# A decoder trunk layer: both feed-forwards by seven products, with the first one's side work cut into steps and its state-space matrices built on GpSimd

## The chip, the cores and the metric

The kernel runs on one core of one Trainium2 chip. The metric is the device time of one execution, in microseconds (us). Engines are called as the profile calls them: PE is TensorE (PEld its weight load), DVE VectorE, ACT ScalarE, POOL GpSimd, SP SyncE, which issues most of the DMAs.

## The reference

One layer with D = 1024, a prompt of 1024 tokens and eight samples of 8 tokens. A feed-forward stands ahead of the token mixer and another behind it:

```python
def swiglu(u, w_in, w_out):
    g, up = jnp.split(u @ w_in, 2, axis=-1)
    return (jax.nn.silu(g) * up) @ w_out
...
    mod = jax.nn.silu(c) @ lp['ada_w'] + lp['ada_b']
    sh1, sc1, g1, sh2, sc2, g2, sh3, sc3, g3 = jnp.split(mod, ADA_CHUNKS, axis=-1)
    h = x + 0.5 * g1[:, None, :] * swiglu(rms_modulate(x, lp['norm_ffn1'], sh1, sc1),
                                          lp['ffn1_w_in'], lp['ffn1_w_out'])
    mix, k, v, sr, si = token_mixer(rms_modulate(h, lp['norm_mix'], sh2, sc2), lp, attend, s0_re, s0_im)
    h = h + g2[:, None, :] * mix
    h = h + 0.5 * g3[:, None, :] * swiglu(rms_modulate(h, lp['norm_ffn2'], sh3, sc3),
                                          lp['ffn2_w_in'], lp['ffn2_w_out'])
```

The mixer has stick-breaking attention and a diagonal complex state-space model (SSM) of 32 groups, 16 channels and 64 states each. The powers and products of the SSM's parameters don't depend on x, so that the kernel can build them at any time before the mixer.

## The kernel before, in words

**Layout.** Activations lie transposed: 1024 features are 8 k-tiles of 128 partitions, and T = 1092 columns hold the prompt, the samples and 4 columns of padding, worked as three chunks of 364 or two halves of 546. Each fp32 product is three f16 passes (high by high, high by low, low by high). A weight block is 1 MB. Class `Weights` fetches it on SP's queue into one of two `wf` buffers, measures it (`absmax`, L89, on DVE, then `partition_all_reduce`, L82, on POOL, then a power of two, L74 to L76), and splits it: the high half on ACT (L101), the low half on DVE (L102). `one_ahead` splits the weights of the next block and loads those of the one after.

**A feed-forward** has 22 inner tiles of 128, in three parts: 0 to 9, 10 to 17, 18 to 21. An *up block* makes one inner tile h (gate and up product, SiLU, product of both). After the up block 10, `down(0)` multiplies the tiles 0 to 9 by their rows of `w_out` and adds to x; then come the up blocks 11 to 21, `down(1)`, and `last_part`.

**The first feed-forward** (`ffn`) uses plain up blocks: `unit` (L216), 144 matmuls of 364 columns. Tiles 0 and 1 are made by chunks beside the modulation of x (`up_two`). x stays in SBUF, and `down` adds to it. Its `fill` puts work of others between the blocks: `ada_part` for the parts 2 to 8 of the modulation, one in each of the blocks 0 to 6 (eight 512 KB weight tiles, issued on POOL's queue at L285, then 32 narrow matmuls at L289); `reload`, which fetches x again; `prep0`, the SSM's parameters, at block 8; and `ssm_prep(bt)` for the four quarters of the SSM's matrices at the blocks 13, 15, 17 and 19, with its elementwise work on DVE (`cmul`, L766 to L775, and L937). Its tiles share one pool `hp` of 15 slots with h.

**The second feed-forward** (`ffn_seven`) makes only the tiles 0 to 3 by plain blocks (`halves_unit`, L242). For the other 18, it cuts weights (256 inner columns) and u into 2x2 quarters and takes seven products of quarters, in place of eight, with sums formed before and after (`seven_products`, L455: 168 matmuls of 272 or 274 columns). The sums of the weights are made on DVE (`seven`, L162 to L165), those of u once, by `Factors.sums` (L430, L431), from the fp32 values kept in x's space. x itself goes to DRAM (`xd`); `down(0)` fetches it row by row and writes it back, and after the last up block it is loaded whole into u's space.

**Order.** The framework plans the program when it is built: each engine's instructions stand then in one fixed order. A tile whose pool is full waits for the release of a slot.

Of the kernel before, what the change touches and what calls it, by code (L numbers as in the profile page):

```python
# [20 lines left out]
P = 128  # L21
# [10 lines left out]
CH = 364  # L32
# [60 lines left out]
def abs_bound(k, src, out):  # L93

    junk = k.tmp().rearrange("p a n -> p (a n)").bitcast(BF16)[:, :src.shape[1]]
    k.nc.scalar.activation(junk, src, AF.Abs, accum_out=out)
# [9 lines left out]
class Weights:  # L106
# [48 lines left out]
    def seven(self, f, s):  # L155
# [4 lines left out]
        t, t4 = (k.tmp().rearrange("p a n -> p (a n)") for _ in range(2))  # L160
        s3, s2, s4 = t[:, :512], t[:, 512:1024], t4[:, :512]
# [115 lines left out]
def ada_part(k, dr, part, queue=None, then=None):  # L277

    nc = k.nc
    ps = k.pss.tile([P, 256], F32, tag="s")  # L280
    for kk in range(2):
        ws = []
        for i in range(4):
            wt = k.hp.tile([P, 4, 256], F32, tag="h", name="aw")
            (queue or nc.gpsimd).dma_start(wt, dr["ada_w"][part, kk, i])  # L285
            ws.append(wt)
        for j in range(4):
            for i in range(4):
                nc.tensor.matmul(ps[32 * i:32 * i + 32, :], k.cs[:, 4 * kk + j, :], ws[i][:, j, :],  # L289
                                 start=kk + j == 0, stop=kk == 1 and j == 3)  # L290
        if kk == 0 and then:
# [8 lines left out]
    nc.vector.tensor_tensor(view(k.mods[:, sl, :]), pt[:, :, :, :NSQ],  # L300
                            view(k.ada_b[:, sl].unsqueeze(2).to_broadcast([P, 8, NSQ])), op=ALU.add)

# [108 lines left out]
class Factors:  # L411

    def __init__(self, k, u):
        self.u, self.t = u, []

    def sums(self, k, x, g):
# [15 lines left out]
    def get(self, n):
        if n[0] == "b":
            k0, c0 = 4 * int(n[1] == "2"), HT * int(n[2] == "2")
            return lambda kt, part: self.u[:, k0 + kt, part, c0:c0 + HT]
        i, j = {"t1": (0, 0), "t3": (0, 1), "t2": (1, 0), "t4": (1, 1)}[n]
        return lambda kt, part: self.t[2 * kt + i][:, j, part]


def seven_products(k, w, fac, iv, h, meanwhile):
# [17 lines left out]
    u2 = k.u2.tile([P, HT], F32, tag="u2", bufs=2)  # L460
# [61 lines left out]
def ffn_order(wi, wo, seven=False):  # L522
    o = [(wi[i], KD, 256, *(("seven",) if seven and i >= PLAIN else ())) for i in range(NFF)]
# [6 lines left out]


def ffn(k, x, u, ivu, gate, fill, after_chunk, between=None):

    nc = k.nc
    hs, hm = {}, {}
    act = lambda kt, part: u[:, kt, part, :]

    def up(i):
        w = k.w.next()
        iv = mul_small(k, w[1], ivu)  # L540
        pg = unit(k, w, slice(0, P), act, KD)
        sil = k.tp.tile([P, T], F32, tag="sil", bufs=2)
        nc.scalar.activation(c3(sil), pg, AF.Silu, scale=iv)
        pu = unit(k, w, slice(P, 2 * P), act, KD)
        h = k.hp.tile([P, T], F32, tag="h")
        nc.vector.scalar_tensor_tensor(c3(h), pu, iv, c3(sil), op0=ALU.mult, op1=ALU.mult)  # L546
        p = [a <= i < b for a, b in PARTS].index(True)
        if p not in hm:
            hm[p] = k.small.tile([P, 12], F32, tag="hm", bufs=3)
        j = i - PARTS[p][0]  # L550
        absmax(k, h, hm[p][:, j:j + 1])
        hs[i] = h
        for f in fill.get(i, ()):
            f()

    def up_two():

        ws = [k.w.ready.pop(0) if between else k.w.next() for _ in range(2)]
        ivs = [mul_small(k, w[1], ivu) for w in ws]
        sil = [k.tp.tile([P, T], F32, tag="sil", bufs=2) for _ in range(2)]  # L560
        hm[0] = k.small.tile([P, 12], F32, tag="hm", bufs=3)
        behind = None
        for i in range(2):
            hs[i] = k.hp.tile([P, T], F32, tag="h")
        for c in range(3):
            for i in range(2):
                ps = k.psu.tile([P, 3, 512], F32, tag="u", bufs=k.nunits)
                for q in range(2):
                    product(k, ps[:, q, :CH], ws[i], slice(q * P, q * P + P), act, KD, c)
                a, b = c3(sil[i])[:, c], c3(hs[i])[:, c]  # L570
                with k.tc.issue_after(behind) if behind else nullcontext():
                    g = nc.scalar.activation(a, ps[:, 0, :CH], AF.Silu, scale=ivs[i])
                b = nc.vector.scalar_tensor_tensor(b, ps[:, 1, :CH], ivs[i], a, op0=ALU.mult, op1=ALU.mult)
                behind = between(c, i, g.ins, b.ins) if between else None
        for i in range(2):
            absmax(k, hs[i], hm[0][:, i:i + 1])
            for f in fill.get(i, ()):
                f()

    def halves(p):  # L580
        a, b = PARTS[p]
        s, inv = pow2_scale(k, allmax(k, absmax(k, hm[p][:, :b - a])), tag="sh", bufs=3)
        parts = []
        for i in range(a, b):
            h2 = k.hp.tile([P, 2, T], F16, tag="h")
            ins = split(k, h2[:, 0, :], h2[:, 1, :], hs[i], s)
            if i - a < 6:
                behind = ins
            parts.append(h2)
        return lambda kt, part: parts[kt][:, part, :], inv, behind  # L590

    def down(p, hact, inv, behind):
        nk = PARTS[p][1] - PARTS[p][0]
        per = 1 + p
        for m in range(KD):
            if m % per == 0:
                if m == 0:
                    with k.tc.issue_after(behind):
                        w = k.w.next()
                else:  # L600
                    w = k.w.next()
                iv = mul_small(k, w[1], inv)
            ps = unit(k, w, slice(m % per * P, m % per * P + P), hact, nk)
            add_gated(k, x[:, m, :], ps, scaled_gate(k, gate[:, m, :], iv))

    up_two()
# [1214 lines left out]
```

## Time and profile before

| what | value |
|---|---|
| time, median of 3 runs | 2479.41 us (2475.33 to 2481.81) |
| profiled execution | 2487.87 us, of which the span of the trace is 2485.9 us |
| mean granted TensorE clock | 0.983 of full speed |
| busy share of the span | PE 96%, DVE 63%, PEld 62%, ACT 35%, POOL 7% |

All times of single instructions come from the profiled execution. Stretches are given in microseconds from the span's start. "x" is a count, and what stands in square brackets behind a row of a timeline is the engine's idle time before the instruction and what ended it.

### The profile page before, as it was taken

To read this page: it belongs to the slowest core of one execution; us is meant where nothing else is said; L and a number is where in the kernel's file an instruction comes from. 1 tells how busy PE (TensorE), PEld (TensorE's weight loads), DVE (VectorE), ACT (ScalarE), POOL (GpSimd) and SP (SyncE) were. 2 spreads that over 40 slices of the span, in tenths; PEclk is the share of its full clock that TensorE was granted. 3 is DMA by queue.
4 is the path that set the end of the run, shared out by engine and by line. 5 is a ranking of instruction groups with operands and counts; after the bars stand their busy time and mean duration, and the time that the engine had idled before them with its cause. 6 is when DMAs were issued, how large, how long until landed. Compare 5 with 4: busy or idle time off the path is not lost.

```text
span 2485.9 us, 40892 instructions
## 1 busy us (share of the span) xinstructions
PE 2389.5 (96%) x17575; PEld 1550.6 (62%) x17575; DVE 1558.6 (63%) x2895; ACT 866.8 (35%) x1049; POOL 171.1 (7%) x249
## 2 busy tenths in 40 slices
PE   6999999999999999999999999999999999999997
PEld 2555566666656566685444444556678878888784
DVE  4522373458675753747889787597477645777735
ACT  3311130111122332236677677332433321333303
POOL 0111000000000000001133300000000000000000
PEclk8999999999999999899999999999999999999999
DMA  9654111212121225445233312622111133111302
GB/s 352 216 193 170 33 50 51 68 55 80 70 71 52 100 88 150 119 132 195 70 109 104 97 42 102 219 73 105 42 39 65 33 133 107 61 54 66 124 18 73
DMA packets 88533, 247.45 MB, mean 100 GB/s; under 512 B 12112, under 2 KB 49360, under 8 KB 78112
## 3 DMA queue, kind: packets, MB, share of 16 engines
q1 hardware_dynamic: 74528, 197.85, 23.6%
q0 software_dynamic: 13376, 46.70, 5.4%
q8 instruction: 137, 2.24, 0.4%
q14 instruction: 44, 0.36, 0.0%
q10 hardware_dynamic: 448, 0.29, 0.0%
HBM read 199.62 MB, written 45.19 MB: 98 GB/s over the span
## 4 chain that ended last, share of the span: by engine, by line
PE 39%; DVE 8%; ACT 4%; DMA 2%; issue 2%; another core or an unknown queue 1%; POOL 0%; DVEq 0%; POOLq 0%; ACTq 0%
PE u L455 13%; PE u L242 9%; PE u L226 8%; PE u L216 3%; PE z L1123 2%; PE o L1141 1%; PE P L1060 1%; DVE wl L102 1%; DVE mx L89 1%; PE P L1136 1%; DMA wf<-in_ffn_w_in 1%; DVE h L102 1%; DMA wf<-in_w_in 1%; DMA wf<-in_w_out_b 0%
## 5 line engine op out<-in xcount | busy, mean ns | idle before, releaser
L216 PEld LDWEIGHTS <-wh 128*128 128x128 f16 x3360 | 320.9, 97 | 225.4 <-issue 38.0
L226 PE MATMUL u<-u,wh 128*128 128x364 f16 (+1 forms) x1632 | 392.7, 318 | 11.1 <-ACT u L389 6.3
L216 PE MATMUL u<-u,wh 128*128 128x364 f16 (+1 forms) x2112 | 392.6, 317 | 0.0
L101 ACT ACTIVATE wh<-wf,sc 128x2048 f16<-128x2048 f32 (+2 forms) x110 | 177.3, 1613 | 540.6 <-PE u L216 308.1
L89 DVE TENSOR_REDUCE mx<-wf 128x1 f32<-128x2048 f32 (+2 forms) x116 | 209.9, 1823 | 201.0 <-DMA wf<-in_ffn_w_in 112.6
L226 PE MATMUL u<-u,wl 128*128 128x364 f16 (+1 forms) x816 | 259.7, 318 | 1.1 <-DVE wl L102 1.1
L226 PEld LDWEIGHTS <-wh 128*128 128x128 f16 x1824 | 175.9, 98 | 123.9 <-issue 26.6
L102 DVE SCALAR_TENSOR_TENSOR wl<-wf,sc,wh 128x2048 f16<-128x2048 f32 (+2 forms) x110 | 204.7, 1861 | 50.7 <-ACT wh L101 48.4
L216 PEld LDWEIGHTS <-wl 128*128 128x128 f16 x1680 | 163.3, 98 | 96.8 <-issue 2.8
L216 PE MATMUL u<-u,wl 128*128 128x364 f16 (+1 forms) x1056 | 220.7, 315 | 0.0
L242 PE MATMUL u<-h,wh 128*128 128x274 f16 (+1 forms) x1152 | 184.4, 281 | 8.5 <-ACT h L101 7.8
L82 POOL PARTITION_ALL_REDUCE am<-mx x106 | 52.3, 499 | 1930.4 <-DVE mx L89 1869.2
L216 PE MATMUL u<-h,wh 128*128 128x364 f16 (+1 forms) x864 | 157.3, 317 | 5.2 <-DVE h L102 3.5
L242 PEld LDWEIGHTS <-wh 128*128 128x128 f16 x1408 | 137.5, 98 | 38.4 <-issue 9.5
L226 PEld LDWEIGHTS <-wl 128*128 128x128 f16 x912 | 89.0, 98 | 69.0 <-issue 18.0
L455 PEld LDWEIGHTS <-wh 128*128 128x128 f16 x1152 | 112.9, 98 | 24.4 <-issue 1.1
L546 DVE SCALAR_TENSOR_TENSOR h<-u,iv,sil 128x1092 f32<-128x1092 f32 x20 | 27.1, 1354 | 143.3 <-PE u L216 108.9
L242 PE MATMUL u<-h,wl 128*128 128x272 f16 (+1 forms) x576 | 114.7, 280 | 0.0
L226 PEld LDWEIGHTS <-aside 128*128 128x128 f16 x864 | 83.0, 97 | 50.3 <-issue 1.2
L455 PEld LDWEIGHTS <-w3h 128*128 128x128 f16 x864 | 84.3, 98 | 21.3 <-issue 3.9
L455 PE MATMUL u<-fac,w3h 128*128 128x272 f16 x576 | 92.1, 281 | 3.1 <-ACT fac L430 2.8
L455 PE MATMUL u<-fac,wh 128*128 128x272 f16 x576 | 91.8, 281 | 0.8 <-ACT fac L430 0.8
(435 smaller groups left out, 3870.7 us busy)
## 6 DMA issues: line engine op xcount, KB each, us to landing
wf<-in_ffn_w_in SPq DMA_DIRECT2D x44, 1024.0 KB, 4.8
aw<-in_ada_w POOLq DMA_DIRECT2D x56, 512.0 KB, 7.0
wf<-in_w_in SPq DMA_DIRECT2D x16, 1024.0 KB, 5.3
wf<-in_ffn_w_out_a SPq DMA_DIRECT2D x16, 640.0 KB, 4.0
x<-in_xT SPq DMA_DIRECT2D x6, 1456.0 KB, 13.4
xd<-x SPq DMA_DIRECT2D x6, 1456.0 KB, 5.9
sg<-gd SPq DMA_DIRECT2D x16, 546.0 KB, 3.6
aw<-in_ada_w SPq DMA_DIRECT2D x16, 512.0 KB, 8.8
```

Source lines behind the costliest of these rows:

```text
L82: k.nc.gpsimd.partition_all_reduce(r, m, P, ABSMAX)
L89: k.nc.vector.tensor_reduce(m, src, axis=axis, op=ALU.max, apply_absolute_value=True)
L101: r = k.nc.scalar.activation(hi, src, AF.Copy, scale=s)
L102: k.nc.vector.scalar_tensor_tensor(lo, src, s, hi, op0=ALU.mult, op1=ALU.subtract)
L216: k.nc.tensor.matmul(ps[:, c, :n], wt[:, cols], act(kt, part)[:, c * CH:c * CH + n], start=kt == 0 and j == 0, stop=kt == nk - 1 and j == 2)
L226: k.nc.tensor.matmul(ps[:, :n], wt[:, cols], act(kt, part)[:, c * CH:c * CH + n], start=kt == 0 and j == 0, stop=kt == nk - 1 and j == 2)
L242: k.nc.tensor.matmul(ps[:, a:b], wt[:, cols], act(kt, part)[:, a0 + a:a0 + b], start=kt == 0 and j == 0, stop=kt == nk - 1 and j == 2)
L455: nc.tensor.matmul(t[:, c0:c1], wt[:, kt * P:kt * P + P], act(kt, part)[:, c0 - 240:c1 - 240], start=first and kt == 0 and j == 0, stop=kt ...
L546: nc.vector.scalar_tensor_tensor(c3(h), pu, iv, c3(sil), op0=ALU.mult, op1=ALU.mult)
L1060: nc.tensor.matmul(acc[:rk, h, :], k.tri[:rk, :rk], part[:, h, :], start=first and j == 0, stop=True, skip_group_check=True)
L1123: nc.tensor.matmul(ps[:, :n], a[r, P * j:P * j + P], b[r, cols], start=i == 0, stop=True, skip_group_check=True)
L1136: nc.tensor.matmul(acc[:, h, q0:], k.earlier, part[:, h, :], start=False, stop=True, skip_group_check=True)
```

## The change

Both feed-forwards now run through one function, made from `ffn_seven`: tiles 0 to 3 plain, 18 by seven products. For the first one this means:

- x's space on the right side of SBUF is closed after the sums and opened again as a pool of 8 slots for h of the tiles 4 to 17 (`XSpace`); before `down(1)` it becomes x again, loaded from `xd`. The 16-bit halves of the tiles 10 to 17 go into u's space. The factor t4 is written over the quarter of u that it replaces (`replace`). The second feed-forward takes this over, with 16 slots in `hp` for 17; the first has 14 for 15.
- The modulation's parts 2 to 8 go in steps of one k-tile: one 512 KB tile, 4 matmuls; three steps in each up block from block 0 on, in a pool of 2 slots of their own.
- `prep0` runs in `down(0)`, `ssm_prep(bt)` in the up blocks 11, 13, 15 and 17 behind `one_ahead`, and its elementwise operations stand on GpSimd in place of VectorE.
- `reload` is gone; the rows for `down(0)` come from the input.

```diff
-def ada_part(k, dr, part, queue=None, then=None):
+def ada_steps(k, dr, part, tile, queue, then=None):
...
-    for kk in range(2):
-        ws = []
+    for kt in range(KD):
+        wt = tile()
+        queue.dma_start(wt, dr["ada_w"][part, kt])
         for i in range(4):
...
+            nc.tensor.matmul(ps[32 * i:32 * i + 32, :], k.cs[:, kt, :], wt[:, i, :], start=kt == 0, stop=kt == KD - 1)
...
+        if kt < KD - 1:
+            yield
...
+    def replace(self, k):
+
+        for g, src in enumerate(self.last):
+            hi, lo = (self.u[:, 2 * g:2 * g + 2, i, HT:] for i in range(2))
+            k.nc.scalar.activation(hi, src, AF.Copy)
+            k.nc.vector.tensor_sub(lo, src, hi)
...
-def ffn_seven(k, fac, ivu, gate, xu, xd, after_sums, after_chunk):
+def ffn(k, fac, ivu, gate, xu, row_of, xd, after_sums, again, fill, after_chunk, between=None):
...
+    def slot(i, shape, dt, name):
+        return (k.hp if i < 4 or i >= PARTS[2][0] else hq).tile(shape, dt, tag="h", name=name)
...
             def meanwhile():
                 if waiting:
                     bound(waiting.pop())
                 k.w.one_ahead()
+                filled(i)
...
+    fac.replace(k)
+    hq = after_sums()
     for i in range(PLAIN, PARTS[0][1] + 1):
         up(i)
     bound(waiting.pop())
-    down(0, *halves(0), row)
+    down(0, *halves(0, lambda i: slot(i, [P, 2, T], F16, "h2")), row)
     for i in range(PARTS[0][1] + 1, NFF):
         up(i)
     bound(waiting.pop())
-    x = k.up.tile([P, KD, T], F32, tag="u", name="x")
+    u2 = k.up.tile([P, KD, 2, T], F16, tag="u", name="h2")
+    h1 = halves(1, lambda i: u2[:, i - PARTS[1][0]])
+    x = again().tile([P, KD, T], F32, tag="x")
     for m in range(KD):
         nc.sync.dma_start(x[:, m, :], xd[:, m, :])
-    h1, h2 = halves(1), halves(2)
-    down(1, *h1, lambda m, _: (x[:, m, :], lambda: None))
+    h2 = halves(2, lambda i: slot(i, [P, 2, T], F16, "h2"))
+    down(1, *h1, lambda m: (x[:, m, :], lambda: None))
     last_part(k, x, gate, *h2, lambda c: after_chunk(c, x))
...
-def cmul(nc, pool, out_r, out_i, ar, ai, br, bi, shape, tag, neg_i=False):
-
+def cmul(nc, pool, out_r, out_i, ar, ai, br, bi, shape, tag, neg=None, e=None):
+
+    e = e or nc.vector
     t = pool.tile([P] + list(shape), F32, tag=tag)
-    nc.vector.tensor_mul(out_r, ar, br)
-    nc.vector.tensor_mul(t, ai, bi)
-    nc.vector.tensor_sub(out_r, out_r, t)
+    e.tensor_mul(out_r, ar, br)
+    e.tensor_mul(t, ai, bi)
...
 def ssm_prep(k, dr, sp, par, bt, ds):
 
     nc = k.nc
+    e = nc.gpsimd
...
+        def ada():
+            for _ in range(3):
+                next(steps, None)
+
+        fill = {i: [ada] for i in range(NFF)}
+        fill[-3] = [prep0]
         for bt in range(4):
-            fill[13 + 2 * bt] = [lambda bt=bt: ssm_prep(k, dr, sp, par[0], bt, ds)]
...
+            fill[11 + 2 * bt] = [ada, lambda bt=bt: ssm_prep(k, dr, sp, par[0], bt, ds)]
```

## Rows read from the trace of the kernel before

**Rows 1.** The page's first part: busy time, share of the span, instructions.

```profile
PE 2389.5 (96%) x17575; PEld 1550.6 (62%) x17575; DVE 1558.6 (63%) x2895; ACT 866.8 (35%) x1049; POOL 171.1 (7%) x249
```

**Rows 2.** Windows: stretch, length, five engines' busy time, clock, DMA share, GB/s.

```profile
97.10:349.90 252.80, 251.82 (x1766) 141.92 (x1765) 89.90 (x232) 35.90 (x32) 26.51 (x54) 1.00 0.36 131
349.90:463.80 113.90, 111.55 (x724) 69.98 (x723) 59.32 (x95) 19.46 (x17) 2.86 (x8) 1.00 0.19 62
463.80:728.20 264.40, 263.35 (x1738) 161.21 (x1736) 171.70 (x601) 42.70 (x35) 4.36 (x12) 1.00 0.20 69
728.20:820.60 92.40, 89.55 (x578) 55.83 (x577) 57.44 (x80) 22.10 (x15) 5.69 (x5) 1.00 0.20 65
1796.10:1987.60 191.50, 187.60 (x1563) 153.24 (x1561) 137.19 (x201) 70.92 (x85) 6.94 (x11) 0.97 0.14 48
1987.60:2109.30 121.70, 115.25 (x962) 94.28 (x961) 61.63 (x105) 22.36 (x20) 3.21 (x8) 0.97 0.35 123
2109.30:2325.80 216.50, 216.50 (x1851) 179.50 (x1849) 157.73 (x231) 78.14 (x96) 4.26 (x12) 1.00 0.17 59
2325.80:2418.20 92.40, 90.34 (x770) 74.38 (x768) 48.56 (x65) 22.02 (x18) 2.03 (x3) 1.00 0.22 80
```

**Rows 3.** Timeline of ACT: the SiLU of two plain up blocks in succession.

```profile
475.27 1.17 ACT L543 ACTIVATE sil<-u,iv 128x1092 f32<-128x1092 f32 x1 [9.52 <-PE u L216]
...
497.48 1.17 ACT L543 ACTIVATE sil<-u,iv 128x1092 f32<-128x1092 f32 x1 [9.52 <-PE u L216]
```

**Rows 4.** Timeline of PE: the modulation's matmuls, two records to a matmul.

```profile
170.40 1.91 PE L289 MATMUL s<-aw,cs 128*32 128x256 f32 x26
```

**Rows 5.** Groups of POOL, shapes apart: busy us, mean ns, idle before, releaser.

```profile
L82 POOL PARTITION_ALL_REDUCE am<-mx x106 | 52.3, 499 | 1930.4 <-DVE mx L89 1869.2 <-DVE x L516 31.8 <-DVE scs L829 22.3
...
L285 POOL DMA_DIRECT2D aw<-in_ada_w x56 | 29.8, 538 | 21.7 <-PE s L289 20.6 <-issue 0.2
...
L1299 POOL TENSOR_SCALAR_AFFINE_SELECT mask_s<-mask_s 64x512 bf16<-64x512 bf16 x1 | 1.1, 1108 | 0.0
...
masks.py:199 POOL TENSOR_SCALAR_AFFINE_SELECT ident<-ident 128x128 f32<-128x128 f32 x1 | 0.3, 285 | 7.4 <-issue 7.4
L1290 POOL TENSOR_SCALAR_AFFINE_SELECT sel<-sel 128x8 f32<-128x8 f32 x1 | 0.2, 223 | 2.7 <-DVE sel L1288 2.7
```

**Rows 6.** Groups of DVE with shapes apart, 463.80 to 728.20: elementwise work of `ssm_prep`.

```profile
L937 DVE TENSOR_TENSOR q<-ct 128x1024 f32<-128x1024 f32 x4 | 4.9, 1220 | 0.0
...
L766 DVE TENSOR_TENSOR wk<-wk 128x4 f32<-128x4 f32 x23 | 3.5, 154 | 0.0
```

**Rows 7.** Timeline at 739: a reduction on POOL and an operation of DVE.

```profile
738.90 2.34 DVE L102 SCALAR_TENSOR_TENSOR wl<-wf,sc,wh 128x2048 f16<-128x2048 f32 x1
...
739.15 2.31 POOL L82 PARTITION_ALL_REDUCE am<-mx  x1 [19.76 <-DVE mx L89]
```

**Rows 8.** Groups of DVE with two SBUF inputs, 2109.30 to 2325.80.

```profile
L102 DVE SCALAR_TENSOR_TENSOR wl<-wf,sc,wh 128x1024 f16<-128x1024 f32 (+1 forms) x21 | 27.9, 1329 | 0.1
L102 DVE SCALAR_TENSOR_TENSOR w3l<-tmp,sc,w3h 128x1024 f16<-128x1024 f32 (+1 forms) x20 | 20.1, 1011 | 0.0
L483 DVE SCALAR_TENSOR_TENSOR h<-q,iv,h 128x1092 f32<-128x1092 f32 x10 | 13.6, 1356 | 1.0
...
L164 DVE TENSOR_TENSOR tmp<-wf 128x512 f32<-128x512 f32 x10 | 6.9, 692 | 0.3
```

**Rows 9.** Timeline of DVE: the first quarter's factors wait for a slot.

```profile
366.18 0.30 DVE L767 TENSOR_TENSOR ct<-cc,pw 128x144 f32<-128x144 f32 x1
...
530.87 1.35 DVE L546 SCALAR_TENSOR_TENSOR h<-u,iv,sil 128x1092 f32<-128x1092 f32 x1 [8.99 <-PE u L216]
532.14 0.30 DVE L766 TENSOR_TENSOR ca<-cc,pw 128x144 f32<-128x144 f32 x1
```

**Rows 10.** Timeline of POOL, then of ACT: measure and split in a seven-product block.

```profile
2165.15 0.36 POOL L82 PARTITION_ALL_REDUCE am<-mx  x1 [19.18 <-DVE mx L89]
...
2168.54 1.15 ACT L101 ACTIVATE wh<-wf,sc 128x1024 f16<-128x1024 f32 x1 [0.98 <-PE u L455]
```

More of the change, by code (lines that the diff above doesn't have):

```diff
@@ L274, in seq_bc @@
     return t.unsqueeze(2).to_broadcast([P, NB, LS])
-def ada_part(k, dr, part, queue=None, then=None):
+def ada_steps(k, dr, part, tile, queue, then=None):
     nc = k.nc
     ps = k.pss.tile([P, 256], F32, tag="s")
-    for kk in range(2):
-        ws = []
+    for kt in range(KD):
+        wt = tile()
+        queue.dma_start(wt, dr["ada_w"][part, kt])
         for i in range(4):
[L284 to L291, printed above, removed]
+            nc.tensor.matmul(ps[32 * i:32 * i + 32, :], k.cs[:, kt, :], wt[:, i, :], start=kt == 0, stop=kt == KD - 1)
+        if kt == 3 and then:
             then()
+        if kt < KD - 1:
+            yield
     sb = k.tp.tile([P, 256], F32, tag="ap", bufs=2)
@@ L519, with ffn_order @@
 PLAIN = 4
-def ffn_order(wi, wo, seven=False):
-    o = [(wi[i], KD, 256, *(("seven",) if seven and i >= PLAIN else ())) for i in range(NFF)]
+def ffn_order(wi, wo):
+    o = [(wi[i], KD, 256, *(("seven",) if i >= PLAIN else ())) for i in range(NFF)]
     a, b, c = wo
@@ L529, in ffn_order @@
     return o[:n] + oa + o[n:] + ob + [(c, 4, D, True)]
[L532 to L606, printed above, removed]
-    for i in range(2, PARTS[0][1] + 1):
-        up(i)
-    down(0, *halves(0))
-    for i in range(PARTS[0][1] + 1, NFF):
-        up(i)
-    h1, h2 = halves(1), halves(2)
-    down(1, *h1)
-    last_part(k, x, gate, *h2, after_chunk)
@@ L651, in ffn_seven, with filled @@
     act = lambda kt, part: fac.u[:, kt, part, :]
+    waiting = []
+    def slot(i, shape, dt, name):
+        return (k.hp if i < 4 or i >= PARTS[2][0] else hq).tile(shape, dt, tag="h", name=name)
+    def filled(i):
+        for f in fill.get(i, ()):
+            f()
     def bound(i):
@@ L683, in up @@
             bound(i)
+            filled(i)
     def up_two():
-        ws = [k.w.next() for _ in range(2)]
+        ws = [k.w.ready.pop(0) if between else k.w.next() for _ in range(2)]
         ivs = [mul_small(k, w[1], ivu) for w in ws]
         for i in range(2):
-            hs[i] = k.h_slot(i, [P, T], F32, "h")
+            hs[i] = slot(i, [P, T], F32, "h")
+        behind = None
         for c in range(3):
@@ L696, in up_two, with halves @@
                 h = c3(hs[i])[:, c]
[L697 to L698 removed]
+                with k.tc.issue_after(behind) if behind else nullcontext():
+                    g = nc.scalar.activation(h, ps[:, 0, :CH], AF.Silu, scale=ivs[i])
+                b = nc.vector.scalar_tensor_tensor(h, ps[:, 1, :CH], ivs[i], h, op0=ALU.mult, op1=ALU.mult)
+                behind = between(c, i, g.ins, b.ins) if between else None
         for i in range(2):
             bound(i)
[L702 removed]
+            filled(i)
+    def halves(p, tile):
         a, b = PARTS[p]
@@ L716, in down @@
         per = 1 + p
-        last = [behind, behind]
         for m in range(KD):
@@ new lines, in trunk_kernel, with __init__, open, x @@
+    class XSpace:
+        def __init__(self, n):
+            self.n, self.i, self.stack = n, 0, ExitStack()
+        def open(self, **kw):
+            self.stack.close()
+            self.i += 1
+            return self.stack.enter_context(again(name=f"xp{self.n}{self.i}", side="right", **kw))
+        def x(self):
+            return self.open(bufs=1)
+        def h(self):
+            return self.open(bufs=8)
+    xs = XSpace(1)
+    with open_pool(tc, name="pss1", bufs=2, space=PSUM) as k.pss, \
@@ L1638, in trunk_kernel @@
         box = {}
-        def reload():
-            for c in range(3):
-                nc.sync.dma_start(x[:, :, c * CH:(c + 1) * CH], dr["xT"][c])
         def prep0():
```

224 lines of the change are left out of this document (116 added, 108 removed).

## The prediction, on record before the change was built

> **What bounds the kernel now.** The page's first part comes first: PE is busy for 96% of the span [rows 1], and the next engine, DVE, for 63%. The time is therefore PE's work, and an edit pays where it shortens PE's stream or fills one of its gaps. The windows by stage come second [rows 2]. The first feed-forward's four stretches, from its block 2 to the end of `down(1)`, have 99% of PE's time filled: 252.8, 113.9, 264.4 and 92.4 us. The same stages of the second one take 191.5, 121.7, 216.5 and 92.4. In each the granted clock is 0.97 or 1.00, so that the difference is not the clock's. The reader is to see two things there: the up blocks are shorter by seven products, and `down(0)` is longer. Third is the period of a plain block, 497.48 − 475.27 = 22.21 us [rows 3]; that of a seven-product block is 216.5/11 = 19.68 [rows 2].
>
> **The change part by part; first the up blocks.** The blocks 2 to 21 cost 20 x 22.21 = 444.2 us before, without the modulation and the SSM's matrices. As in the second feed-forward, they should take 191.5 + 216.5 = 408.0, which has its two plain blocks and the making of the factors in it. That is **−36.2**.
>
> **down(0).** 121.7 for 113.9 [rows 2], of which 6.45 are idle PE (121.7 − 115.25): **+7.8**.
>
> **down(1), in both feed-forwards.** The halves of the tiles 10 to 17 now go into u's space, and the last product of block 21 still reads u. So their eight splits (0.73 of ACT ahead, then about 1.36 of DVE each, the price of a two-input operation of 1092 columns [rows 8]) start behind block 21 and not beside it. The first k-tile is ready some 3.8 us later, counting the last tile's product, and PE then follows the splits one by one. The ends are nothing (PE has other work, `down(1)` starts with tiles that are ready) and 11 us each (8 x 1.36, all bare). I take 4 each, since PE needs longer for a k-tile than a split takes: **+8**. The reload of x stands behind the release of the eight slots, but its first row is wanted only when the first half product of `down(1)` is done, 92.4/16 = 5.8 us later.
>
> **Modulation.** Seven parts cost 252.8 − 9 x 22.21 = 52.9, 7.5 each, or 0.94 for a k-tile [rows 2, 3]. Where 13 matmuls run in one piece they take 1.91 [rows 4], so that three steps together would take 1.76 and a part 4.7. The ends are no gain (steps stay apart) and −20. I take **−9**, a bit under half, since a pool of two slots has one step wait for its tile now and then.
>
> **Elementwise work of the SSM's matrices, DVE to GpSimd.** One quarter has 135 operations with 12,900 elements a partition. On DVE 4 elements took 154 ns and 1024 took 1220 [rows 6], a line of 0.150 us + 1.045 ns per element: 33.7 us. DVE was no limit there (171.7 of 264.4 us busy [rows 2]), so taking that off gives nothing by itself. PE needs for two blocks 39.4, plus 5.0 of the matrices' own products ((264.4 − 11 x 22.21)/4), plus about 4.6 of modulation: 49.0. GpSimd needs for two blocks p for the quarter, 6 x 0.54 for the modulation's DMAs and 2 x 0.36 for reductions [rows 5, 10]: p + 3.9. No row shows an elementwise product of GpSimd. Below, p is DVE's own 33.7. In the middle it is 36, by the select of 128 columns (0.22 us + 0.5 ns per element, from 223 and 285 ns [rows 5]); above it is 52, by that of 512 columns (1.76 ns per element, from 1108 ns).
>
> To that come waits. At 739 a reduction that takes 0.36 elsewhere took 2.31, and ended with the DVE operation beside it [rows 7, 10]. DVE spends 8.3 us of a seven-product block in operations with two SBUF inputs (27.9 + 20.1 + 13.6, four sums of 6.9 and some 2.7 of halves, over 11 blocks [rows 8]): 16.6 in two blocks, if each holds GpSimd up. What is queued behind a late quarter is the reduction of a weight block, and behind that its scale, its split and PE. The cushion is some 11 us, once: the scale is there 2.4 us before the split begins [rows 10], and the split is done 9 us before PE wants it. So there is a stall of 4 x (p + waits − 45.1) − 11 us. With p = 36 and half the waits it is nothing; with all of them it is 19. I take **+6**. The ends are 0 and, with p = 52 and all waits, 83.
>
> The Trainium skill's page "GPSIMD Engine Reference" (§ 3, Performance versus the Vector engine) states that a product of two fp32 tensors takes GpSimd 1.96 times as long as VectorE, 4497 against 2293 ns for 2048 columns. By that p would be an estimated 66 us and the stall some 73 without any wait; no row here shows such an operation. Its page "SBUF — State Buffer" (Who interferes with whom) says that a VectorE operation with two SBUF inputs and a GpSimd operation shut each other out; the reduction of 2.31 us agrees.
>
> **At nothing.** The start (the same matmuls, in other tiles) and the lead of the norm's coefficients. t4 is written over u in place of a slot of its own, in the plain block 3, as work of ACT and DVE beside PE; bare, it would cost 2 x 1.3. `prep0` moves from block 8 to `down(0)`, where DVE has 54 of 114 us free. The reload of 4.4 MB on SP goes, and eight rows come from the input in its stead, at a DMA share of 0.2.
>
> **Sum.** −36.2 + 7.8 + 8 − 9 + 6 = **−23.4**. The profiled execution took 2487.87 us, of which 2485.9 are the span: 2464.5. The median of the runs stands at 2479.41/2487.87 = 0.9966 of it, so that the forecast is **2456**.
>
> **Rivals.** *GpSimd sets the pace* (the one on the slower side). The fixed order puts a quarter's 135 operations ahead of the reduction of a weight block that is wanted one or two blocks later; GpSimd, 7% busy before [rows 1], becomes a serial part of the weights' loop. For it speak the slope of the 512-column select and the lengthened reduction; against it, that two blocks give 49 us, and p by the 128-column select is 36. It cancels the gain where the stall reaches 29.4, at p + waits = 55.2; at p = 52 with all waits the time is (2464.5 − 6 + 83) x 0.9966 = 2533. The GpSimd page's ratio belongs to this rival: with it alone the time is an estimated 2523.
>
> *The joints eat the gain.* hp has 14 slots for 15, and now holds the factors, the sums and `tmp` too. Slots are given in program order: the first quarter's factors were computed at 366, but the result that needs an hp slot was written only at 532, right behind h of block 13 [rows 9]. If `ca` and `q` wait likewise, and h of a block behind them, or both `down(1)` cost 11, PE stands for another 12 to 25 us: 2468 to 2481, little or no change. Against it speaks that the tiles 4 to 17 left hp.
>
> *Nothing waits and the steps run together.* The joints hide, the modulation gives its 20 and the stall is nothing: −23.4 − 8 − 11 − 6 = −48, or 2431.
>
> *DVE is held up by GpSimd in turn.* Each of its two-input operations waits for one GpSimd operation of about 0.3 us, nine to a block, 2.7 us. DVE has 157.7/11 = 14.3 of 19.7 us busy in a seven-product block [rows 2], so that this fits. Late splits would cost at most that much in the eight blocks beside which the quarters stand, 22 us: about 2478.
>
> **How the numbers follow.** A measurement of this kernel can't tell 0.3% from no change; that is 2472 to 2487. Chances: the forecast, with its own range from 2440 to 2471, 0.43; nothing waits 0.06; GpSimd sets the pace 0.33, spread evenly over stalls of 10 to 83; the joints 0.12; DVE held up 0.06. Of GpSimd's, a sixth (stalls up to 22) still is faster and a fifth (up to 37) the same; of the joints' a third is faster. Faster is 0.43 + 0.06 + 0.05 + 0.04 = 0.58; the same 0.07 + 0.08 + 0.05 = 0.20; slower the rest of GpSimd's and a last 0.01 of DVE's, 0.22. The range goes from 2432, the gain without a joint, to 2520, where the stall is 70. The cases leave some 0.09 outside of it, the upper stalls and half of "nothing waits"; what is left to 0.2 is for causes that I don't name.
>
> **What would show it.** Right: the blocks 11 to 21 at about 19.7 us plus 2.5 where a quarter's products stand; POOL busy some 36 to 50 us per quarter, and its reductions not ahead of an idle PE; gaps of 4 us at both `down(1)`; a `down(0)` near 122. Wrong: PE idle in the blocks 12 to 20 with the chain of waits going through POOL, or operations of GpSimd of over 0.4 us a piece; gaps of more than 10 us at the joints; or h waiting for a slot that `ca` or `q` holds. The prediction falls if p + waits go over 55.

## The result, and the profile after

The changed kernel takes 2584.49 us (median of 4 runs, 2582.16 to 2589.72) against 2477.37 for the kernel before on the same chip: a ratio of 1.0433 (95% interval 1.0409 to 1.0457). The forecast was 2456 with a range from 2432 to 2520. The first part of the page of the changed kernel, and of its 40 slices PE, POOL and PE's granted clock:

```profile
PE 2371.8 (92%) x18535; PEld 1652.1 (64%) x18535; DVE 1619.6 (63%) x2617; ACT 953.2 (37%) x1193; POOL 377.3 (15%) x789
...
PE   5999999675779999999999999999999999999997
...
POOL 0000001467750000000123320000000000000000
PEclk9999999778779999988999999999999999999999
```

PE has less work than before [rows 1] and a hole in the slices 8 to 12. It coincides with POOL's new work, and the granted clock falls there. The windows of the changed kernel, in the order of [rows 2] (same columns), say how much each stage took:

```profile
102.10:327.95 225.85, 206.74 (x1833) 156.95 (x1831) 143.62 (x211) 76.05 (x92) 22.19 (x44) 0.99 0.35 124
327.95:444.39 116.44, 113.27 (x964) 93.18 (x962) 66.37 (x192) 19.31 (x20) 13.19 (x24) 1.00 0.32 108
444.39:844.89 400.50, 292.24 (x2201) 207.49 (x2200) 175.81 (x247) 83.40 (x110) 208.89 (x556) 0.82 0.22 79
844.89:937.03 92.14, 90.44 (x767) 74.33 (x767) 60.17 (x83) 25.35 (x20) 6.25 (x6) 1.00 0.32 118
1903.70:2086.90 183.20, 182.87 (x1561) 151.31 (x1560) 138.89 (x203) 73.06 (x86) 7.06 (x11) 1.00 0.18 61
2086.90:2203.20 116.30, 113.37 (x964) 93.16 (x962) 59.49 (x103) 21.03 (x19) 4.15 (x8) 1.00 0.33 110
2203.20:2420.97 217.77, 216.79 (x1851) 179.38 (x1850) 155.72 (x231) 77.51 (x95) 4.24 (x12) 1.00 0.16 57
2420.97:2513.10 92.13, 90.42 (x767) 74.32 (x767) 50.05 (x66) 23.36 (x19) 3.02 (x3) 1.00 0.22 84
```

One stage has the whole loss: the blocks 11 to 21 of the first feed-forward take 400.5 us where they took 264.4 [rows 2]. The others are shorter than before, or longer by 2.5 us at most. POOL's timeline in that stretch shows what the prediction had not priced (in brackets, the idle time before the instruction and what ended it; "issue" is time in which the engine waited for nothing that the profile shows):

```profile
451.37 0.41 POOL L82 PARTITION_ALL_REDUCE am<-mx  x1 [7.44 <-issue]
458.67 0.40 POOL L711 TENSOR_TENSOR ct<-pw,bb 128x128 f32<-128x128 f32 x1 [6.90 <-issue]
459.05 0.19 POOL L711 TENSOR_TENSOR wt<-wk 128x4 f32<-128x4 f32 x1
...
469.55 0.41 POOL L82 PARTITION_ALL_REDUCE am<-mx  x1 [6.14 <-issue]
476.85 0.43 POOL L710 TENSOR_TENSOR ca<-cc,pw 128x144 f32<-128x144 f32 x1 [6.90 <-issue]
477.24 0.74 POOL L283 DMA_DIRECT2D aw<-in_ada_w  x1
```

Each time that GpSimd goes from elementwise work to the all-reduce, or back, 5.8 to 7.6 us pass. Between 398.79 and 786 this happens 23 times, for 154.2 us of idle time named "issue". With 216.4 us of busy time (the fifth after the comma in the window below) that is 370.6 of 387.2 us, 96%. Such a stand is called a load from here on, since a load of code is the reading that the experiments set out from; what GpSimd does in it no trace shows.

```profile
398.79:786.00 387.21, 281.94 (x2131) 199.84 (x2129) 159.80 (x227) 71.23 (x93) 216.42 (x571) 0.82 0.24 84
```

The waits of the same stretch (in total, times, longest us), PE's and SP's queue's among them, show three roads from there to PE:

```profile
PE s L285 <- DMA aw<-in_ada_w: 50.2, 11, 17.4
...
DVE sc L74 <- POOL am L82: 37.2, 8, 11.8
...
PE s L834 <- ACT ct L835: 25.3, 3, 11.7
```
```profile
SPq L122 <- DVE s L165: 116.0, 6, 23.2
SPq L888 <- POOL ct L887: 115.9, 4, 35.5
```

The modulation's tiles come late, since GpSimd issues them; so do the scales of the weight blocks; and SP stands before the store of a quarter's last result (L888), with the next weight fetch (L122) in its order behind it.

### The profile page after: what moved, and what is told of

It is laid out like the page before. It is cut to its first block, busy times and chain, and to the rows that moved or that the text cites. A ratio compares the mean times of both kernels' runs of the same rounds, so it can differ in the third digit from the quotient of the medians.

```text
span 2580.4 us, 43245 instructions
## 1 busy us (share of the span) xinstructions
PE 2371.8 (92%) x18535; PEld 1652.1 (64%) x18535; DVE 1619.6 (63%) x2617; ACT 953.2 (37%) x1193; POOL 377.3 (15%) x789
## 4 chain that ended last, share of the span: by engine, by line
PE 40%; DVE 6%; ACT 3%; DMA 2%; issue 1%; POOL 0%; DVEq 0%; POOLq 0%; ACTq 0%
PE u L470 13%; PE u L242 9%; PE u L226 8%; PE u L216 2%; PE z L1069 2%; PE o L1087 1%; PE P L1006 1%; DVE mx L89 1%; PE P L1082 1%; DVE wl L102 1%; PE z L1130 1%; DMA wf<-in_w_in 1%; ACT x L385 0%; DVE mh L102 0%; DMA wf<-in_ffn_w_out_a 0%
## 5 line engine op out<-in xcount | busy, mean ns | idle before, releaser
L226 PE MATMUL u<-u,wh 128*128 128x364 f16 (+1 forms) x1632 | 393.4, 320 | 9.5 <-ACT u L387 6.3
L242 PE MATMUL u<-h,wh 128*128 128x272 f16 (+1 forms) x2304 | 365.7, 279 | 11.5 <-DVE h L102 7.8
L101 ACT ACTIVATE wh<-wf,sc 128x1024 f16<-128x1024 f32 (+2 forms) x128 | 182.2, 1426 | 431.5 <-PE u L242 175.3
L89 DVE TENSOR_REDUCE mx<-wf 128x1 f32<-128x1024 f32 (+2 forms) x134 | 211.0, 1597 | 157.5 <-DMA wf<-in_ffn_w_in 90.9
L470 PE MATMUL u<-u,wh 128*128 128x272 f16 x1728 | 284.7, 287 | 12.1 <-DVE q L491 9.6
L226 PE MATMUL u<-u,wl 128*128 128x364 f16 (+1 forms) x816 | 260.6, 320 | 1.1 <-DVE wl L102 1.1
L102 DVE SCALAR_TENSOR_TENSOR wl<-wf,sc,wh 128x1024 f16<-128x1024 f32 (+2 forms) x128 | 210.1, 1642 | 64.6 <-ACT wh L101 63.7
L470 PE MATMUL u<-fac,w3h 128*128 128x272 f16 (+1 forms) x1152 | 188.9, 285 | 9.2 <-DVE xr L506 5.7
L470 PE MATMUL u<-u,wl 128*128 128x272 f16 x864 | 176.2, 286 | 0.0
L470 PE MATMUL u<-fac,w3l 128*128 128x272 f16 x576 | 116.9, 284 | 0.0
```

The source lines that it names most:

```text
L89: k.nc.vector.tensor_reduce(m, src, axis=axis, op=ALU.max, apply_absolute_value=True)
L101: r = k.nc.scalar.activation(hi, src, AF.Copy, scale=s)
L102: k.nc.vector.scalar_tensor_tensor(lo, src, s, hi, op0=ALU.mult, op1=ALU.subtract)
L226: k.nc.tensor.matmul(ps[:, :n], wt[:, cols], act(kt, part)[:, c * CH:c * CH + n], start=kt == 0 and j == 0, stop=kt == nk - 1 and j == 2)
L242: k.nc.tensor.matmul(ps[:, a:b], wt[:, cols], act(kt, part)[:, a0 + a:a0 + b], start=kt == 0 and j == 0, stop=kt == nk - 1 and j == 2)
L470: nc.tensor.matmul(t[:, c0:c1], wt[:, kt * P:kt * P + P], act(kt, part)[:, c0 - 240:c1 - 240], start=first and kt == 0 and j == 0, stop=kt ...
```

## The experiments

The chips differ by some 0.5% (the kernel before ran at 2479 to 2492 us beside these runs), so that only ratios to the kernel before are compared. "Stretch" is the time from PE's last product of `down(0)` to its first of `down(1)` in the first feed-forward, from each run's timeline of PE.

| run | edit | ratio (interval) | stretch, us |
|---|---|---|---|
| before | | 1 | 264.4 |
| changed kernel | | 1.0433 (1.0409 to 1.0457) | 400.5 |
| 1 | elementwise work on VectorE | 0.9940 (0.9918 to 0.9961) | 276.9 |
| 2 | copies for reductions | 1.0305 (1.0280 to 1.0330) | 375.6 |
| 3 | modulation's tiles on SP | 1.0331 (1.0305 to 1.0357) | 390.9 |
| 4 | before, with loads alone | 0.9996 (0.9980 to 1.0012) | 264.4 |
| 5 | 2 and 3 | 1.0086 (1.0062 to 1.0110) | 338.4 |
| 6 | 1, quarters spread | 0.9905 (0.9875 to 0.9934) | 266.1 |
| 7 | 6, steps two and one | 0.9849 (0.9825 to 0.9874) | 254.1 |
| 8 | 3, maximum by TensorE | 1.0305 (1.0283 to 1.0327) | 374.5 |
| 9 | two stores on GpSimd's queue | 1.0475 (1.0458 to 1.0493) | 412.1 |
| 10 | 8, transfers off SP | 1.0052 (1.0033 to 1.0071) | 316.7 |
| 11 | 10, steps two and one | 1.0020 (1.0005 to 1.0034) | 313.8 |
| 12 | before, quarters on GpSimd | 1.0313 (1.0292 to 1.0334) | 344.0 |
| 13 | 10, reductions back on GpSimd | 1.0324 (1.0307 to 1.0341) | 406.1 |
| 14 | 10, copies for reductions | 1.0110 (1.0081 to 1.0138) | 339.5 |
| 15 | 7, tiles on SP | 0.9717 (0.9683 to 0.9750) | 244.3 |

**1. The part undone.**

```diff
-    e = nc.gpsimd
+    e = nc.vector
```

> The changed kernel with the elementwise work of the SSM's matrices back on VectorE, at the same places. Theory A (GpSimd loads code, some 7 us, each time it goes from the all-reduce to elementwise work or back): no gaps of that size left on POOL between the start of down(0) and block 21. Theory B (the elementwise operations themselves, 46 to 48 us a quarter, are too long for GpSimd): the same, since they are gone. Both: the stretch of the blocks 11 to 21, 398 us in the changed kernel, falls to between 255 (what PE needs) and 300 (VectorE's 157 us of the second feed-forward plus 135 of the four quarters); the time to between 2440 and 2487 us. It tells what all else in the change is worth.

0.9940: the elementwise work's place is worth 4.9% of the time before (1.0433 − 0.9940), and all else in the change, taken together, is a small gain. POOL has no gap of that size left between `down(0)` and block 21. PE stands for 19.4 us of the stretch (276.9 − 257.5), with VectorE busy for 237.6, in the window of run 1:

```profile
448.94:725.88 276.94, 257.49 (x2201) 193.50 (x2200) 237.63 (x741) 84.10 (x110) 16.89 (x33) 0.99 0.31 110
```

**2. No reductions, so no loads.** In `allmax`, from `down(0)` to block 21 of the first feed-forward:

```diff
+    if getattr(k, "probe", False):
+        k.nc.gpsimd.tensor_copy(r, m)
+        return r
```

> The changed kernel, but from down(0) to block 21 of the first feed-forward the maximum over the partitions of a weight block is left out: a plain copy of each partition's own maximum on GpSimd stands in the place of the all-reduce, in the same queue with the same waits. The elementwise work stays on GpSimd. Theory A: the 24 code loads of the stretch go, and with them nearly all of the loss; blocks 11 to 21 in 255 to 290 us, the time 2440 to 2480 us. Theory B: the elementwise work still takes 46 to 48 us a quarter ahead of the copies, so that at least half of the loss of some 140 us stays: over 2515 us.

1.0305, so that more than half of the loss stays, as theory B had it. But its reason is not the one that theory B gave. The loads are gone, and PE now waits 93 us for the modulation's tiles, up to 28.7 at a time, and GpSimd waits 76.5 for PE to free a tile's slot. A quarter runs in one piece of 45 us, with the next tile's issue behind it. Theory A, as the only cause, fell.

**3. Tiles on SP.** The queue in `modulation()` is `nc.sync`.

> The changed kernel with the modulation's weight tiles issued on SP's queue and not on GpSimd's, all else the same. Theory C (PE stands in its own order before the modulation's matmuls, because their tiles are issued late behind GpSimd's other work: 50 us of PE's waits in the blocks 11 to 21): these waits go, the time falls by 40 to 50 us to 2535 to 2545. Theory A: the loads stay in front of the weights' reductions and of the matrices too, so that PE waits there in place of it: a gain under 25 us, 2560 to 2585.

1.0331, a gain of some 1%, between the two. But it doesn't lie where theory C had it: the stretch is hardly shorter (390.9), and the blocks 2 to 10 are (210.7 us from their first step to `down(0)`, for 225.6). The late tiles are no sole cause of the loss either.

**4. Loads without work.** In the kernel before, ahead of the all-reduce:

```diff
+        t = k.small.tile([P, 1], F32, tag="mx", bufs=8)
+        k.nc.gpsimd.tensor_single_scalar(t, m, 1.0, op=ALU.mult)
+        m = t
```

> The kernel before, and from down(0) to block 21 of the first feed-forward one GpSimd operation more ahead of each reduction: the 128x1 maximum times 1.0, which gives the same value. Theory A: 6 to 7 us of gap between this operation and the reduction, 19 times, and a second load hidden in the wait before it; the weights' chain has some slack, so the time goes up by 0 to 40 us (2477 to 2517). Theory B: operations of 0.2 us, no gap, no change of the time: within 0.2% of 2477.

The gap is there, as POOL's timeline of this run shows, and the time stays (0.9996):

```profile
504.80 0.27 POOL L84 TENSOR_SCALAR mx<-mx 128x1 f32<-128x1 f32 x1 [12.52 <-DVE mx L93]
510.90 0.41 POOL L86 PARTITION_ALL_REDUCE am<-mx  x1 [5.84 <-issue]
```

One of the two loads of a round hides in the wait for VectorE's maximum: the operation at 504.80 starts 0.1 us behind that maximum's end. The other's 5.9 us fit the slack of the weights' chain. So a load costs nothing here, with a GpSimd that is mostly idle (176.8 of 2488 us busy).

**5. Both.**

> The copy in place of the all-reduce (as before it leaves out the maximum over the partitions in that stretch) and the modulation's tiles on SP's queue, together; the elementwise work stays on GpSimd. Theory A (code loads) alone gave back 1.2 of 4.3 per cent, theory C (late tiles) alone 1.0, so neither holds by itself. Theory D: three kinds of things that PE wants stand in GpSimd's one order among a quarter's 42 us of operations, and either of two is enough to make PE wait; with both gone most of the loss is gone: ratio to the kernel before 0.982 to 0.998, blocks 11 to 21 in 255 to 280 us. Theory B (the elementwise work is too long for GpSimd in any case, as the copies and PE's own products of the matrices still stand behind it): at least half of the loss stays, ratio over 1.015.

1.0086, between the theories' ranges: 3.5 of the 4.3 per cent are back, more than the 2.3 of both alone. PE still waits 48.2 us for tiles, now behind SP's wait for a quarter's store. That led to the runs 8 to 10.

**6 and 7. VectorE, spread.**

```diff
+        fill[4] = [ada, prep0]
+        for bt, i in enumerate((7, -3, 13, 17)):
+            fill[i] = fill.get(i, []) + [lambda bt=bt: ssm_prep(k, dr, sp, par[0], bt, ds)]
```

> The elementwise work on VectorE, as in the first experiment (0.994 of the kernel before), but the parameters at block 4 and the quarters at block 7, in down(0), and at the blocks 13 and 17, where VectorE has room. If the first experiment's blocks 11 to 21 (274 us for some 255 of PE's work) were held up by VectorE: these fall to 250 to 260, and the blocks 4 to 10 grow by less than 6: ratio 0.984 to 0.991. If not (the loss there is PE's own gaps and clock): 0.992 to 0.997, as in the first experiment.

0.9905, in the range of the first reading, but the trace bears out the second: VectorE had not held the stretch up. The stretch fell from 276.9 to 266.1 us, by 10.8, and PE's busy time in it by 10.2, which is the products of the two quarters that now stand elsewhere. PE's idle time stayed (266.1 − 247.3 = 18.8 for 19.4), although VectorE has 43 us less to do. The gain is that the blocks 2 to 10 take in a quarter and grow no longer (from block 2's first step to `down(0)` 231.7 us in both runs).

```profile
454.22:720.31 266.09, 247.30 (x2119) 189.63 (x2117) 194.84 (x471) 81.64 (x105) 17.17 (x33) 0.98 0.28 101
```

Then two steps of the modulation stand in `meanwhile`, and one behind `seven_products` (`fill[100 + i]`, `ada(1)`):

> The same, and of the modulation's three steps in a seven-product block two stand in its middle and one at its end. In the changed kernel a step waits 2 to 3 us for its tile in each of the blocks 4 to 10, with two slots and a tile that takes some 4 us to land. If that is what the gap is, it goes: 0.3 to 0.7 per cent less than the run above. If the third step only waits elsewhere: within 0.2 per cent of it.

0.9849, about half a per cent less. The groups of PE from 160 to 720 (busy, mean ns of one | idle before), of run 6 and then of run 7:

```profile
L285 PE MATMUL s<-aw,cs 128*32 128x256 f32 x376 | 27.3, 389 | 21.1 <-DMA aw<-in_ada_w 21.1
```
```profile
L285 PE MATMUL s<-aw,cs 128*32 128x256 f32 x360 | 26.5, 393 | 0.6 <-DMA aw<-in_ada_w 0.6
```

PE's wait for the third tile of a block is gone, and the stretch stands at 254.1 us, with 9.0 of them idle:

```profile
452.14:706.25 254.11, 245.13 (x2121) 188.51 (x2120) 194.47 (x475) 81.25 (x104) 16.55 (x34) 0.99 0.30 106
```

**8. Maximum by TensorE.** In place of the copy of run 2, with the tiles on SP:

```diff
+        nc.tensor.transpose(ps[:1, :P], m, k.ident)
...
+        nc.vector.tensor_reduce(t[:1], ps[:1, :P], axis=AX.X, op=ALU.max)
+        nc.tensor.matmul(ps[:, P:P + 1], k.ones[:1, :], t[:1], start=True, stop=True)
+        nc.vector.tensor_copy(r, ps[:, P:P + 1])
```

> The elementwise work on GpSimd, the modulation's tiles on SP, and from down(0) to block 21 the maximum over partitions by a transpose on TensorE, a maximum on VectorE and a product with ones, so that nothing of the weights' chain stands in GpSimd's order and nothing is left out. Theory D: as without the reductions, plus at most 1.5 us of PE waiting for its own little product at each of some 20 maxima: ratio 0.985 to 1.008. Theory B: over 1.015, with PE waiting for the matrices.

1.0305, against theory D, and over theory B's bound without its reason, since PE waits only some 6 us for the matrices' factors. The waits from 438 to 812, first SP's, then others:

```profile
SPq L900 <- POOL ct L899: 106.7, 4, 28.5
```
```profile
DVE mx L98 <- DMA wf<-in_ffn_w_in: 96.9, 8, 22.6
...
PE pmax L85 <- DVE mx L98: 44.7, 6, 21.2
```

SP stands before the quarter's store, the weights come late behind it, and PE, which now takes part in the maximum, waits in its own order.

**9. Stores alone.** `ds["ca"]` and `ds["ph"]` are written on GpSimd's queue.

> The changed kernel; only the stores of two of a quarter's results (the chunk powers ph and the factors ca, made by GpSimd) are issued by GpSimd itself, behind the operation that makes them, and no longer on SP's queue. Theory E: SP stands up to 35 us, 116 us in all, before the store of ph, and the next weight block's fetch is the next thing in its order; this is one of three ways on which a late quarter reaches PE. Then SP's waits for ct and ca go, and 1 to 2.5 per cent of the time with them (ratio 1.018 to 1.033); reductions and modulation tiles still stand in GpSimd's order. If SP's waits are only shadows of the reductions' lateness: within 0.4 per cent of the changed kernel, 1.039 to 1.047.

1.0475: no gain, though SP has no such store to wait for any more. It now stands 186.3 us before weight fetches for VectorE's sums (L122), where it stood 116.0. While GpSimd is full, opening this road to PE alone doesn't help.

**10 and 11. Nothing behind a quarter.** Run 8 with `ca`, `ph` and the load of `cc` on GpSimd's queue, `m1` and `gp` on ScalarE's; then with the steps of run 7.

> The elementwise work on GpSimd; the modulation's tiles on SP; the maximum over partitions by TensorE and VectorE from down(0) to block 21; and all of a quarter's transfers off SP's queue (those behind GpSimd's results on GpSimd's, those behind ScalarE's on ScalarE's). Nothing is left out of the computation. Theory E: nothing that PE wants for the up blocks stands behind a quarter any more, only the matrices' own products do; without the last of these measures it was 1.0305: now 0.985 to 1.005. Theory B (the elementwise work is too long for GpSimd at 42 to 48 us a quarter for every 49 us): PE still waits for the matrices' products, over 1.012.

> The same with the modulation's three steps as two and one, which was worth 0.55 per cent with the elementwise work on VectorE: 0.3 to 0.7 per cent less than the run above. If it beats 0.985, GpSimd is the better place for this work, and the loss was all in the order of the queues.

1.0052 at the upper end of theory E, and 1.0020. What run 8 lost is mostly back, but it doesn't reach VectorE's 0.9940 or 0.9849. GpSimd stays nearly full in the windows of run 10 (POOL's busy time is the fifth after the comma):

```profile
480.00:540.00 60.00, 54.03 (x427) 37.39 (x425) 32.11 (x45) 15.29 (x23) 55.67 (x127) 0.91 0.32 118
540.00:600.00 60.00, 48.17 (x353) 31.54 (x352) 28.95 (x42) 12.28 (x16) 52.62 (x115) 0.82 0.33 116
600.00:660.00 60.00, 54.65 (x435) 37.90 (x433) 32.60 (x47) 16.71 (x22) 57.21 (x135) 0.93 0.32 113
```

GpSimd is busy for 165.5 of 180 us without any load: elementwise work alone nearly fills it, as theory B says. But the time is below theory B's 1.012, and PE's waits for GpSimd's results come to only 9.9 us of the stretch. Of the 39.7 us that the stretch has over run 1, 27.8 are busy time of PE (285.3 for 257.5). The maximum's own products are 7.9 of that, and its clock is 0.91 for 0.99. The other 12 are idle time. What part of it is GpSimd's is not shown.

**12. The part alone, in the kernel before.** `cmul` and `ssm_prep` of the changed kernel in the old one.

> The kernel before with one part of the change alone: the quarters' elementwise work on GpSimd, at the blocks 13, 15, 17 and 19 as it was. No modulation stands in that stretch. Theory E with the code loads: reductions behind the quarters and weight fetches behind the store of ph still hold PE: 1.015 to 1.045. If it takes the modulation's tiles in the same order to make the loss: within 0.5 per cent of no change.

1.0313: most of the loss is there with no modulation near it, with 14 loads of 91.1 us in the stretch. PE waits three times some 16 us for the quarter's factors:

```profile
608.12 0.63 PE L914 MATMUL s<-ca,bb 64*32 64x128 f32 x2 [16.28 <-POOL ca L769]
```

**13 and 14. Loads or order.** Run 10 with the all-reduce on GpSimd, and with the copy of run 2.

> As the tenth experiment (modulation's tiles and a quarter's transfers off the queues in which they stood behind a quarter), but with the reductions on GpSimd as in the changed kernel, code loads and all. In the changed kernel GpSimd is busy for 216 us and loads for 154 of the 387 us between its first and last load, 96 per cent. Theory F: GpSimd's time is what sets the length of this stretch, and the loads are the larger part of what the prediction left out; then all the other measures change nothing, the stretch stays at 370 to 400 us, and the ratio is 1.035 to 1.048. If the order of queues made the loss and the loads only fill idle time: 1.005 to 1.02.

> The same with plain copies in GpSimd's order in place of the reductions: no code loads, but each weight block's scale still stands behind a quarter's operations (the maximum over partitions is left out from down(0) to block 21). Theory F: GpSimd has some 220 us of work for a stretch of 255 and the planner's order lets the copies in between: 1.000 to 1.010, as with the maximum made by TensorE (1.005). If the reductions' place in GpSimd's order is itself what costs: 1.015 to 1.03.

Run 13 has 1.0324: close below what theory F gave, with a stretch of 406.1 us, a little over its 370 to 400. GpSimd has 222.7 us of work and 160.9 of "issue" in 380 to 780, 96% again:

```profile
380.00:780.00 400.00, 282.06 (x2184) 203.79 (x2182) 157.81 (x238) 74.23 (x96) 222.73 (x565) 0.82 0.22 82
```

Run 14 has 1.0110, a little above what theory F gave. There the scales wait for GpSimd's order (79.5 us in VectorE's waits), without a load.

**15. The best of both.** Run 7, and the modulation's tiles on SP's queue.

> The seventh experiment's kernel (elementwise work on VectorE, quarters spread, steps two and one: 0.9849) with the modulation's tiles on SP's queue. In the runs with the tiles on SP the blocks 2 to 10 took some 17 us less than with GpSimd's queue (208.5 for 225.9 in the changed kernel); if that is the tiles' lateness, most of it is gone already by two and one (PE's wait for them fell from 21.9 to 5.6 us), and only up to 8 us are left: 0.981 to 0.985. If SP's queue has the tiles ready together, so that three steps run in one piece: 0.976 to 0.980. If the weight fetches suffer behind the tiles: over 0.986.

0.9717, better than any of the three had it: 2414.25 us against 2483.82 on the same chip. The windows from its block 2's first step to `down(0)`, and those of run 7:

```profile
99.24:317.60 218.36, 209.63 (x1873) 158.49 (x1872) 181.76 (x483) 78.47 (x98) 5.32 (x11) 1.00 0.39 135
```
```profile
102.09:333.00 230.91, 215.75 (x1873) 160.99 (x1872) 181.98 (x483) 78.34 (x98) 21.97 (x43) 0.97 0.37 128
```

These blocks take 12.5 us less, and the stretch behind `down(0)` has 244.3 us for 254.1. PE stands idle less in them (8.7 of 218.4 us for 15.2 of 230.9), and its granted clock is 1.00 for 0.97. PE's wait for the tiles themselves, from 100 to 720, fell only from 5.6 to 2.1 us, so that most of this gain is not the tiles' lateness at PE. What else GpSimd's 56 issues had cost was not tried. This kernel beats both the kernel before and the changed one.

## Why the prediction was wrong

**The step that failed** is GpSimd's bill for two blocks, "p + 3.9". It has a price for the operations and for waits, but none for the change between two kinds of GpSimd's work. The changed kernel's trace puts 154 us there, 38.5 a quarter. The prediction's own formula then gives 4 x (49.6 + 38.5 − 45.1) − 11 = 161 us of stall; PE's own parts of the stretch are 216.5 + 20.1 for four quarters + 23 steps x 0.94 = 258, so that 400.5 is a stall of 142. The two are near each other partly by luck. Without the loads the same formula leaves 4 x (49.6 − 45.1) − 11 = 7 us, and run 14, which has none, still has a stall of 339.5 − 258 = 81. So a second step failed too, the cushion of "some 11 us, once". In run 14 only the road that the prediction did price is left, a weight block's scale behind a quarter, and VectorE waits for it nine times, up to 24.0 us. The roads by the late tiles and by SP's stores have no price in the prediction at all.

The rival "GpSimd sets the pace" named the mechanism, with the wrong reason and too low a price (83 at most).

A sign was there: at the start of the kernel before, ahead of its first select, GpSimd stood for "7.4 <-issue 7.4" [rows 5], and the prediction read only the 285 ns beside it. The Trainium skill has a rule that may stand behind this ("GPSIMD Engine Reference", § 2.1 Instruction dispatch): the first call of a freshly loaded kernel on GpSimd pays an instruction load of about 6 us that no instruction in the profile shows. The traces agree in size, with 5.8 to 7.6 us at the changes of kind; that each change loads code again is an inference that no run here shows.

**What the loss consists of**, by the stretch: taking the loads out is worth 406.1 − 339.5 = 67 us (runs 13 and 14), the reductions' place in the order 339.5 − 316.7 = 23 (14 and 10), and VectorE for GpSimd 316.7 − 276.9 = 40 (10 and 1). Only the first is a clean pair. The runs 14 and 10 differ in what makes the maximum as well, and the runs 10 and 1 in that and in the queues. Run 1 keeps 19 more than PE's 258; its longest named wait there is 6.5 us, for the modulation's tiles. The other roads, tiles and stores, are worth little while the loads stand (390.9, 412.1 and 406.1 for 400.5). Once the loads are gone, each is enough to keep PE waiting (375.6, 374.5, 338.4). So the parts can't be added up from runs that change one thing.

A part of it is clock: in the changed kernel's stretch PE is busy for 292.2 us, with a granted clock of 0.82, and in run 1 for 257.5 with the same matmuls at 0.99. So some 35 us are slower work, and 108 idle time (400.5 − 292.2). The clock of the stretch is a mix of the two levels, 1.00 (2.4 GHz) and 0.50 (1.2 GHz). At 447.5 PE stands still for 5.65 us, waiting for VectorE; in windows of 2 us, the clock behind that is 0.50 from 454 to 458, with PE busy all the time, and 1.00 again from 460. The windows of 12 us show it more coarsely:

```profile
440.00:452.00 12.00, 7.50 (x65) 6.07 (x63) 3.77 (x7) 0.00 (x0) 4.33 (x6) 1.00 0.36 135
452.00:464.00 12.00, 10.85 (x74) 7.30 (x73) 6.15 (x12) 1.66 (x2) 4.42 (x15) 0.72 0.11 47
464.00:476.00 12.00, 0.28 (x2) 0.23 (x2) 5.65 (x11) 3.39 (x4) 0.41 (x1) 0.72 0.04 8
```

**p and the waits:** their sum came near, partly by luck. The quarters took (216.4 − 4.7 of reductions − 13.3 of issues)/4 = 49.6 us; in the kernel before, with fewer operations of VectorE beside them, (350.9 − 171.1)/4 = 44.9 (run 12 against [rows 1]). The prediction had 36 plus half the waits, 44.3, and an upper end of 52 plus waits. By run 12, p alone is nearer to 45 than to 36; what the fuller stretch adds is some 5 us and not 8.3. So p was too low and the waits too high. Prices of the changed kernel, from POOL's groups with shapes apart:

```profile
L883 POOL TENSOR_TENSOR q<-ct 128x1024 f32<-128x1024 f32 x4 | 7.9, 1972 | 0.1
...
L710 POOL TENSOR_TENSOR ct<-pw,bb 128x128 f32<-128x128 f32 x16 | 6.5, 407 | 7.2 <-issue 7.2
```

That is 1.57 us for 896 elements more, or 1.75 ns each: the 512-column select, the far end, was the row to go by. Against VectorE's 1220 ns [rows 6] the ratio is 1.62. The Trainium skill ("GPSIMD Engine Reference", § 3 Performance versus the Vector engine) gives 1.96, for an add of twice the columns; the measured ratio decides here.

**Up blocks:** right. Run 7's stretch, with two of the quarters in it, is 254.1 for 216.5 + 10 + 21.6 = 248. The second feed-forward's blocks 2 to 10 even fell from 191.5, at a clock of 0.97 [rows 2], to 183.2 at 1.00, which the sum did not have. **down(0):** +2.5 in place of +7.8 (116.4 for 113.9). **down(1):** nothing in place of +8 (92.14 and 92.13 for 92.4); the splits hide, the lower end. **Modulation:** no gain in place of −9. The blocks 2 to 10 took 225.9 us with 33 steps in and around them, (225.9 − 191.5)/33 = 1.04 us a step for 0.94 before. The gain was there to be had: with the tiles on SP (run 3) it is (210.7 − 191.5)/33 = 0.58. **Rivals:** no joint cost anything, and among the waits of the stretch there is none of h behind `ca`. VectorE was held up by GpSimd, as the last rival has it: the sum below takes 1645 ns, and 692 in the second feed-forward of the same trace. But VectorE is busy for 175.8 of 400.5 us there, and did not set the pace.

```profile
L163 DVE TENSOR_TENSOR wf<-wf 128x512 f32<-128x512 f32 x10 | 16.4, 1645 | 0.1
```

## What to carry to other kernels

An engine's bill has three columns: its operations, its waits, and what it pays to change from one kind of work to another. Before moving work to an engine that is 7% busy, see which operations of another kind would stand between those moved, and what in its order and in the DMA queues that take its results the bound engine waits for. When taking one road away changes nothing, count the engine's full time first: here it was full for 96%, and with the loads in place no order of queues that was tried shortened the stretch by more than 10 us.

## What the runs showed of the hardware that was not expected

The change between elementwise work and the all-reduce costs GpSimd 5.8 to 7.6 us each way. It can lie within a wait for something else: in run 4 the operation at 504.80 starts 0.1 us after the maximum that it waited for. And GpSimd can stand still beside VectorE's operations with two SBUF inputs, however small its own is. In run 2, on VectorE and then on POOL:

```profile
474.59 1.36 DVE L501 SCALAR_TENSOR_TENSOR h<-q,iv,h 128x1092 f32<-128x1092 f32 x1
475.88 1.49 DVE L105 SCALAR_TENSOR_TENSOR wl<-wf,sc,wh 128x1024 f16<-128x1024 f32 x1
```
```profile
474.61 0.20 POOL L718 TENSOR_TENSOR wk<-wk,wt 128x4 f32<-128x4 f32 x1
474.76 1.25 POOL L723 TENSOR_TENSOR wk<-wk,wt 128x4 f32<-128x4 f32 x1
```

An operation of 4 columns takes 0.20 us where it starts 0.02 us behind VectorE's. The next one, of the same size, takes 1.25 and ends with VectorE's, as the reduction of [rows 7] did. Why the first gets through is not shown.
